# Per-token scales: from identity products into a bank to a DRAM row loaded for every partition

## The chip, the cores and the metric

One core of one Trainium2 chip runs the kernel. The metric is device microseconds of one execution. Three runs of the kernel before gave a median of 2810.96 us (2810.95 to 2812.11). A profile is one further execution, recorded by the hardware profiler.

## The reference

A one-layer encoder block on x of 2048 tokens by 1024 features, in float32. What matters here is where a per-token scale is multiplied in:

```python
def rms_norm(x, g):
    y = xf * lax.rsqrt(jnp.mean(xf * xf, axis=-1, keepdims=True) + NORM_EPS)
    return (y * g).astype(x.dtype)

def hybrid_layer(...):
    xn = rms_norm(x, mix_norm_g)
    proj = xn @ w_in                       # attention, mLSTM and gate inputs
    ...
    x = x + y @ w_out
    hn = rms_norm(x, ffn_norm_g)
    x = x + jnp.square(jax.nn.relu(hn @ w_up)) @ w_down
    return x
```

A last RMSNorm closes the block. The scale of a token is one number, the same for all 1024 features. The kernel keeps features on the 128 partitions and tokens along the free dimension, so it needs the scales of 512 tokens as a row of 512 values, the same in every partition.

## The kernel before

The 2048 tokens are four blocks `b` of T = 512; blocks 0 and 1 form the first span (s = 0), 2 and 3 the second. Matrices are float32, each split into a high and a low part (tiles `r` and `wsp`), and each product is three matmuls of 128x512: L644 to L646 in plain tiles and in the FFN's down projection, L727 and L755 where a two-by-two block scheme with seven products (`quad`) is used. There are 10,680 of these large matmuls. Attention and mLSTM work of smaller shapes (L1344, L1375, L1406, L1630 to L1702) is put between them.

The work is written as generators, each of which says on which engine its next step runs and for how long. `Flow` (L96) runs them against a clock per engine and so sets TensorE's order. `Order` (L225) then takes the finished instructions, keeps TensorE's order, and sets that of VectorE, ScalarE, GpSimd and SP by due times and by when their inputs are ready, with a margin (2.5 us behind a DMA). The result is a fixed order on every engine. All DMAs are issued by SP, one after the other; each takes the next of eight semaphores, and an SP instruction that waits holds up those behind it.

SBUF tiles come from pools: `tmp` (6 tiles of 128x516), `ctx` (16), `bias` (2), `wraw` (4, raw weights) and `wsp` (3, split weights). PSUM has 8 banks (`self.banks`) of 128x512.

Scales are computed as a [128, 4] tile, tokens on partitions: token t·128 + p of a block is at partition p, column t. To turn that into a row in all partitions, the kernel multiplies a column, broadcast to 128x128, with the identity, four times, into one bank. It does so in three places:

- `norm_in` (L1026), for blocks 0 and 1: squares and sums of x, a product with ones (L1059), mean and eps (L1063), power −0.5 on GpSimd (L1067), the four products (L1074). Eight `scale_in` (L1154) then multiply x by gain and row on VectorE (L1161), send the result to DRAM (`xn`) and split it for the block's products.
- `stats_far` and `rows_far` (L1085, L1107), for blocks 2 and 3: the scale is computed from x loaded with tokens on partitions (L1096 to L1105) and kept in `r_far`; later the products (L1115) go into a bank and ScalarE copies it to a `bias` tile (L1118), which the loads of x multiply by (L1788).
- `norm_mid` (L2092) and `residual` (L2174): the FFN's input isn't scaled; the factor (`mid`, L2110) is applied to the residual instead. In each span's down projection, `residual` goes through four groups (half of the features, block h). Per group: four products (L2183) into a bank; then for each of four feature tiles x2 is loaded into a `tmp` tile (L2198), multiplied by the bank (L2200) and added to the accumulator (L2204). The next group starts when the multiplies are done.

The final RMSNorm (`final`, L2239) needs the finished accumulators: squares (L2284), their sum (L2287), a product with ones (L2309), transposes (L2340), and scaled outputs (L2349 on ScalarE or L2351 on VectorE), stored by L2355. `split_now` (L579) splits weights on ScalarE (L583) and VectorE (L585).

Of the kernel before, what the change touches and what calls it, by code (L numbers as in the profile page):

```python
# [28 lines left out]
ALU = mybir.AluOpType  # L29

P = 128
D = 1024
S = 2048
T = 512
# [338 lines left out]
class Layer:  # L373
# [652 lines left out]
    def norm_in(self, b):  # L1026
        fl, nc = self.fl, self.nc
        B = self.blk[b]
        r = self.rr["x"]
        xt, ev = [], [Event() for _ in range(KT)]  # L1030
        if b == 0:
            (tot,) = yield "get", self.ctx, 1
            xt = yield "get", self.ctx, KT
            B["xg"] = yield "get", self.rpool, KT
            B["xs"] = yield "get", self.rpool, KT
            fl.set(B["xs_ev"])
            for k in range(KT):
                fl.spawn(self.square_in(b, k, xt[k], tot, ev), 0)
        else:
            (tot,) = yield "get", self.ctx, 1  # L1040
            for k in range(KT):
                if k > 0:
                    (x,) = yield "get", self.ctx, 1
                else:
                    x = tot
                yield "sp", 900, 2000
                nc.sync.dma_start(x[:, :T], self.io["xt"][b, k])
                yield "act", act_ns(T)
                nc.scalar.square(x[:, :T], x[:, :T])
                if k > 0:  # L1050
                    yield "dve", dve_ns(T)
                    nc.vector.tensor_add(tot[:, :T], tot[:, :T], x[:, :T])
                    fl.put(self.ctx, x)
                fl.set(ev[k])
        yield "wait", ev
        (bk,) = yield "get", self.banks, 1
        yield "pe", 900
        for t in range(NT):
            nc.tensor.matmul(bk[:, 2 * t:2 * t + 2], tot[:, t * P:(t + 1) * P], self.ones,  # L1059
                             start=True, stop=True)  # L1060
        fl.put(self.ctx, tot)
        yield "dve", 75
        nc.vector.tensor_scalar(r, bk[:, :2 * NT].rearrange("p (t a) -> p t a", a=2)[:, :, 0], 1.0 / D, EPS,  # L1063
                                op0=ALU.mult, op1=ALU.add)
        fl.put(self.banks, bk)
        yield "pool", 960
        nc.gpsimd.tensor_tensor(r, r, self.half, op=ALU.pow)  # L1067
        if b == 0:
            fl.set(self.ev_r)
            yield "wait", [self.ev_const]  # L1070
        (bk,) = yield "get", self.banks, 1
        yield "pe", 1080
        for t in range(NT):
            nc.tensor.matmul(bk[:, t * P:(t + 1) * P], r[:, t:t + 1].to_broadcast([P, P]), self.ident,  # L1074
                             start=True, stop=True)
        done = [Event() for _ in range(KT)]
        for k in range(KT):
            if b > 0:
                (x,) = yield "get", self.ctx, 1
                xt.append(x)  # L1080
            fl.spawn(self.scale_in(b, k, xt[k], bk, done[k]), 2)
        yield "wait", done
        fl.put(self.banks, bk)

    def stats_far(self):  # L1085

        fl, nc = self.fl, self.nc
        for b in (2, 3):
            r, q = self.rfar[b - 2], self.rq
            for t in range(NT):  # L1090
                for g in range(2):
                    (x,) = yield "get", self.temp, 1
                    x5 = x[:, :T]
                    yield "sp", 900, 2000
                    row = b * T + t * P
                    nc.sync.dma_start(x5, self.io["x"][row:row + P, g * T:g * T + T])  # L1096
                    yield "act", act_ns(T, ap=1)
                    nc.scalar.activation(x5, x5, AF.Square, accum_out=q[:, g, t:t + 1])
                    fl.put(self.temp, x)
            yield "dve", 75  # L1100
            nc.vector.tensor_add(r, q[:, 0], q[:, 1])
            yield "dve", 75
            nc.vector.tensor_scalar(r, r, 1.0 / D, EPS, op0=ALU.mult, op1=ALU.add)
            yield "pool", 960
            nc.gpsimd.tensor_tensor(r, r, self.half, op=ALU.pow)  # L1105

    def rows_far(self, ready, read):  # L1107

        fl, nc = self.fl, self.nc
        got = yield "get", self.bias, 2  # L1110
        for b in range(2):
            (bk,) = yield "get", self.banks, 1
            yield "pe", 1080
            for t in range(NT):
                nc.tensor.matmul(bk[:, t * P:(t + 1) * P], self.rfar[b][:, t:t + 1].to_broadcast([P, P]),  # L1115
                                 self.ident, start=True, stop=True)
            yield "act", act_ns(512, True)
            nc.scalar.copy(got[b][:, :T], bk)  # L1118
            fl.put(self.banks, bk)
            self.rows[b] = got[b][:, :T]  # L1120
        fl.set(ready)
        yield "wait", read
        fl.put(self.bias, *got)
# [27 lines left out]
            fl.put(self.temp, tmp)  # L1151
        fl.set(ev[k])

    def scale_in(self, b, k, slot, bk, ev):  # L1154
        fl, nc = self.fl, self.nc
        x = slot[:, :T]
        if b > 0:
            yield "sp", 900, 2000
            nc.sync.dma_start(x, self.io["xt"][b, k])
        yield "dve", dve_ns(574)  # L1160
        nc.vector.scalar_tensor_tensor(x, x, self.gcol[:, 0, k:k + 1], bk, op0=ALU.mult, op1=ALU.mult)  # L1161
        fl.set(ev)
        fl.spawn(self.store(self.xnd[b].ap()[k], x, self.xn_kept[b][k]), 2)
        if b > 0:
            B = self.blk[b]
            if k > 0:
                yield "wait", [B["x_room"][k - 1]]
            B["xs"] += yield "get", self.rpool, 1
            fl.set(B["x_room"][k])
            if k == KT - 1:  # L1170
                fl.set(B["xs_ev"])
        yield from self.split(x, self.blk[b]["xs"][k])
        fl.set(self.blk[b]["xn" if b > 0 else "xs_done"][k])
        yield "wait", [self.xn_kept[b][k]]
        fl.put(self.ctx, slot)
# [916 lines left out]
    def norm_mid(self, s, h):  # L2092

        fl, nc, B = self.fl, self.nc, self.blk[2 * s + h]
        (tot,) = yield "get", self.bias, 1
        summed = [Event() for _ in range(KT)]
        yield "wait", B["x2"]
        for j in range(KT):
            (x,) = yield "get", self.sc, 1
            fl.spawn(self.square_mid(s, h, j, x, tot[:, :512], summed), 3)  # L2100
        yield "wait", summed
        (bk,) = yield "get", self.banks, 1
        yield "pe", 900
        for t in range(NT):
            nc.tensor.matmul(bk[:, 2 * t:2 * t + 2], tot[:, t * P:(t + 1) * P], self.ones,
                             start=True, stop=True)
        fl.put(self.bias, tot)
        m, e = self.mid[h], self.mid2[h]
        yield "dve", 75
        nc.vector.tensor_scalar(m, bk[:, :2 * NT].rearrange("p (t a) -> p t a", a=2)[:, :, 0], 1.0 / D, EPS,  # L2110
                                op0=ALU.mult, op1=ALU.add)
        fl.put(self.banks, bk)
        yield "dve", 75
        nc.vector.scalar_tensor_tensor(e, m, EPS, m, op0=ALU.mult, op1=ALU.mult)
        fl.set(B["mid"])

    def square_mid(self, s, h, j, x, tot, summed):
# [56 lines left out]
    def residual(self, s):  # L2174
# [2 lines left out]
        done = []  # L2177
        for o, h in ((0, 0), (4, 1), (0, 1), (4, 0)):
            yield "wait", [self.blk[2 * s + h]["mid"], self.acc_ev[s][o, h]]
            (bk,) = yield "get", self.banks, 1  # L2180
            yield "pe", 432
            for t in range(NT):
                nc.tensor.matmul(bk[:, t * P:(t + 1) * P], self.mid[h][:, t:t + 1].to_broadcast([P, P]),  # L2183
                                 self.ident, start=True, stop=True)
            done = []
            for j in range(o, o + 4):
                yield "wait", [self.acc_ev[s][j, h]]
                (x,) = yield "get", self.temp, 1
                done.append(Event())
                fl.spawn(self.residual1(s, j, h, bk, x, done[-1]), 2)  # L2190
            yield "wait", done
            fl.put(self.banks, bk)

    def residual1(self, s, j, h, bk, x, done):
        V = self.nc.vector
        x5 = x[:, :512]
        yield "sp", 900, 2000
        self.nc.sync.dma_start(x5, self.x2d[2 * s + h].ap()[j])  # L2198
        yield "dve", dve_ns(512)
        V.tensor_mul(x5, x5, bk)  # L2200
        self.fl.set(done)
        a = self.acc[s][j, h][:, :512]
        yield "dve", dve_ns(512)
# [159 lines left out]
    def build(self):  # L2363
# [14 lines left out]
        self.ypd = [f32d(f"yp{b}", KT, P, T) for b in range(NB)]  # L2378
        self.fin = [f32d(f"fin{h}", 4, P, T) for h in range(2)]
        self.ud = f32d("u", 4, 7, 4, P, T)  # L2380
        self.wi = 0
        self.y3 = [{}, {}]
        self.wtile = {}
# [112 lines left out]
```

## Time and profile before

| | |
|---|---|
| median of three runs | 2810.96 us |
| the profiled execution | 2811.24 us |
| its span, first to last instruction | 2809.5 us |
| mean granted TensorE clock | 0.999 |
| moved by DMA | 662.41 MB, mean 236 GB/s |
| HBM read, written | 462.63 MB, 197.13 MB |

How to read the lines that follow. PE is TensorE's matmuls, PEld its weight loads (they overlap with matmuls), DVE is VectorE, ACT ScalarE, POOL GpSimd, SP the queue that issues the DMAs. A group line gives source line, engine, operation, output tile `<-` input tiles, shapes and count, then busy time, the mean of one in ns, and the idle time before with what ended it. A line of the timeline or of the chain begins with start and length in us. A line of the waits has "engine tile line `<-` what it waited for: us in total, times, longest". A view of one source line gives min/median/max in ns, then first and last start. A DMA line ends with KB each and the median us from issue to landing.

### The profile page before, as it was taken

To read this page: it belongs to the slowest core of one execution; us is meant where nothing else is said; L and a number is where in the kernel's file an instruction comes from. 1 tells how busy PE (TensorE), PEld (TensorE's weight loads), DVE (VectorE), ACT (ScalarE), POOL (GpSimd) and SP (SyncE) were. 2 spreads that over 40 slices of the span, in tenths; PEclk is the share of its full clock that TensorE was granted. 3 is DMA by queue.
4 is the path that set the end of the run, shared out by engine and by line. 5 is a ranking of instruction groups with operands and counts; after the bars stand their busy time and mean duration, and the time that the engine had idled before them with its cause. 6 is when DMAs were issued, how large, how long until landed. Compare 5 with 4: busy or idle time off the path is not lost.

```text
span 2809.5 us, 39519 instructions
## 1 busy us (share of the span) xinstructions
PE 2785.5 (99%) x13528; PEld 2331.6 (83%) x13528; DVE 2042.4 (73%) x3742; ACT 1528.2 (54%) x2642; POOL 50.3 (2%) x100
## 2 busy tenths in 40 slices
PE   9999999999999999999999999999999999999998
PEld 7887888888878878888888888888888888888887
DVE  7796789668896866886676788889888644555565
ACT  5564577544354535575555566566645655554444
POOL 0010001000000000000000000000000000000000
PEclk9999999999999999999999999999999999999999
DMA  7957758768756667588878776688687655666563
GB/s 270 290 193 252 225 157 287 242 221 301 244 185 207 239 235 262 187 292 315 290 274 283 262 235 206 222 266 261 206 272 254 210 187 200 218 228 205 191 224 133
DMA packets 317737, 662.41 MB, mean 236 GB/s; under 512 B 35552, under 2 KB 62304, under 8 KB 317536
## 3 DMA queue, kind: packets, MB, share of 16 engines
q1 hardware_dynamic: 317536, 659.90, 70.1%
q8 instruction: 106, 1.74, 0.3%
q14 instruction: 95, 0.78, 0.1%
HBM read 462.63 MB, written 197.13 MB: 235 GB/s over the span
## 4 chain that ended last, share of the span: by engine, by line
PE 95%; DMA 2%; DVE 2%; ACT 1%; issue 1%; SPq 0%; POOLq 0%; DVEq 0%; ACTq 0%
PE bank L727 44%; PE bank L644 12%; PE bank L645 12%; PE bank L646 12%; PE bank L1344 3%; PE bank L1375 2%; PE bank L1406 2%; PE bank L755 2%; DVE wsp L585 0%; PE bank L1667 0%; PE bank L1668 0%; PE bank L2340 0%; PE bank L1669 0%; PE bank L1653 0%; DMA r<-mfar 0%
## 5 line engine op out<-in xcount | busy, mean ns | idle before, releaser
L727 PE MATMUL bank<-r,wsp 128*128 128x512 f32 x5544 | 1263.6, 390 | 1.6 <-ACT r L1182 1.1
L727 PEld LDWEIGHTS bank<-r,wsp 128*128 128x128 f32 x5544 | 1038.6, 188 | 221.1 <-DVE ctx L1834 3.1
L585 DVE TENSOR_TENSOR wsp<-wraw,wsp 128x1024 fp32r<-128x1024 f32 x459 | 561.1, 1223 | 375.3 <-ACT wsp L583 357.6
L583 ACT CAST wsp<-wraw 128x1024 fp32r<-128x1024 f32 x459 | 482.4, 1051 | 498.4 <-PE bank L727 224.8
L644 PE MATMUL bank<-r,wsp 128*128 128x512 f32 x1472 | 590.0, 401 | 1.6 <-ACT r L1180 1.6
L645 PE MATMUL bank<-r,wsp 128*128 128x512 f32 x1472 | 575.8, 391 | 0.4 <-DVE r L1185 0.4
L646 PE MATMUL bank<-r,wsp 128*128 128x512 f32 x1472 | 575.1, 391 | 0.0
L646 PEld LDWEIGHTS bank<-r,wsp 128*128 128x128 f32 x1472 | 276.3, 188 | 59.2
L644 PEld LDWEIGHTS bank<-r,wsp 128*128 128x128 f32 x1472 | 277.0, 188 | 50.0 <-ACT r L1180 2.4
L645 PEld LDWEIGHTS bank<-r,wsp 128*128 128x128 f32 x1472 | 277.2, 188 | 48.4 <-DVE r L1185 1.0
L1834 DVE TENSOR_TENSOR ctx<-bank,ctx 128x512 f32<-128x512 f32 x186 | 127.1, 688 | 100.7 <-PE bank L727 100.5
L1185 DVE TENSOR_TENSOR r<-r 128x512 fp32r<-128x512 f32 x264 | 174.2, 690 | 30.4 <-ACT r L1180 29.1
L1180 ACT CAST r<-r 128x512 fp32r<-128x512 f32 x264 | 157.7, 621 | 56.3 <-DMA r<-u 49.4
L1826 ACT COPY ctx<-bank 128x512 f32<-128x512 f32 x186 | 108.0, 582 | 71.5 <-PE bank L727 67.5
L1390 ACT ACTIVATE sc<-sc,scs 128x640 f32<-128x640 f32 (+4 forms) x128 | 97.5, 763 | 65.8 <-DVE scs L1387 55.7
L2164 ACT ACTIVATE ctx<-ctx 128x512 f32<-128x512 f32 x96 | 60.6, 631 | 100.7 <-DVE ctx L1834 100.7
L1411 DVE TENSOR_TENSOR r<-bank,r 128x512 fp32r<-128x512 f32 (+1 forms) x168 | 96.5, 596 | 17.6 <-ACT r L1409 16.7
L1381 DVE CUSTOM_DVE_ANT_0 sc<-bank,bias 128x320 f32<-128x320 f32 (+3 forms) x240 | 103.3, 462 | 6.2 <-PE bank L1375 4.9
L1344 PE MATMUL bank<-r,r 128*128 128x256 f32 (+1 forms) x672 | 105.9, 279 | 0.2 <-DVE r L1411 0.2
L1344 PEld LDWEIGHTS bank<-r,r 128*128 128x128 f32 x672 | 98.3, 189 | 9.2 <-DVE r L1411 0.5
L1409 ACT CAST r<-bank 128x512 fp32r<-128x512 f32 (+1 forms) x168 | 81.1, 516 | 35.4 <-PE bank L1406 31.0
L602 DVE TENSOR_TENSOR wraw<-wraw,wraw 128x1024 f32<-128x1024 f32 x76 | 92.9, 1223 | 2.0
(247 smaller groups left out, 2764.5 us busy)
## 6 DMA issues: line engine op xcount, KB each, us to landing
wraw<-in_wf SPq DMA_DIRECT2D x178, 512.0 KB, 4.3
wraw<-wsum SPq DMA_DIRECT2D x136, 512.0 KB, 4.1
r<-u SPq DMA_DIRECT2D x224, 256.0 KB, 4.2
wraw<-in_w SPq DMA_DIRECT2D x88, 512.0 KB, 5.0
u<-ctx SPq DMA_DIRECT2D x128, 256.0 KB, 2.5
ctx<-in_wf SPq DMA_DIRECT2D x112, 256.0 KB, 4.6
wsum<-ctx SPq DMA_DIRECT2D x112, 256.0 KB, 4.1
u<-tmp SPq DMA_DIRECT2D x96, 256.0 KB, 3.7
```

What stands on the lines that cost most here:

```text
L583: nc.scalar.copy(w[:, 0], raw)
L585: nc.vector.tensor_sub(w[:, 1], raw, w[:, 0].bitcast(F32))
L644: mm(ps, lh, rh, start=first, stop=False)
L645: mm(ps, lh, rl, start=False, stop=False)
L646: mm(ps, ll, rh, start=False, stop=last)
L727: mm(ps, wv[:, x, k, n], a[:, y], start=new and k == 0 and x == y == 0, stop=k == 3 and x == 1, skip_group_check=True)
L1180: self.nc.scalar.copy(dst[:, 0], src)
L1185: self.nc.vector.tensor_sub(dst[:, 1], src, dst[:, 0].bitcast(F32))
L1344: nc.tensor.matmul(bk[:, c0:c0 + w], st, sl[:, x, o:o + w], start=n == 0, stop=n == total - 1)
L1381: nc.vector.tensor_tensor_reduce(out=e[:, x * w:x * w + w], in0=bks[x][:, :w], in1=br[:, j0 + x * w:j0 + x * w + w], op0=ALU.add, op1=ALU. ...
L1826: nc.scalar.copy(t[:, o:o + 512], ps)
L1834: nc.vector.tensor_add(t[:, o:o + 512], ps, t[:, o:o + 512])
```

## The change

The row no longer goes through TensorE and a bank. The [128, 4] tile is stored to a small DRAM tensor as 512 consecutive values (`row_out`), and the row is loaded into all 128 partitions of an SBUF tile by a DMA whose source has a step of 0 over the partitions (`row_in`). There is one DRAM row for block 1's input scale, one each for blocks 2 and 3, and one for each of the four blocks' `mid`. Block 0 keeps its products. `residual` loads the row anew for each of its groups, into a `tmp` tile that is held until the group's multiplies are done; `norm_in` of block 1 holds one too. `rows_far` loads straight into the `bias` tiles, without a bank and a copy.

```diff
@@ norm_in
-        (bk,) = yield "get", self.banks, 1
-        yield "pe", 1080
-        for t in range(NT):
-            nc.tensor.matmul(bk[:, t * P:(t + 1) * P], r[:, t:t + 1].to_broadcast([P, P]), self.ident,
-                             start=True, stop=True)
+            (bk,) = yield "get", self.banks, 1
+            row = bk
+            yield "pe", 1080
+            for t in range(NT):
+                nc.tensor.matmul(bk[:, t * P:(t + 1) * P], r[:, t:t + 1].to_broadcast([P, P]), self.ident,
+                                 start=True, stop=True)
+        else:
+            yield from self.row_out("in1", r)
+            (bk,) = yield "get", self.temp, 1
+            row = bk[:, :T]
+            yield from self.row_in("in1", row)
...
-        fl.put(self.banks, bk)
+        fl.put(self.banks if b == 0 else self.temp, bk)
+
+    def row_out(self, name, src):
+        yield "sp", 500, 2000
+        self.nc.sync.dma_start(self.rowd[name].ap().rearrange("(t p) -> p t", p=P), src)
+
+    def row_in(self, name, dst):
+        yield "sp", 900, 2000
+        self.nc.sync.dma_start(dst, bass.AP(self.rowd[name], 0, [[0, P], [1, T]]))
@@ stats_far
             nc.gpsimd.tensor_tensor(r, r, self.half, op=ALU.pow)
+            yield from self.row_out(f"in{b}", r)
@@ rows_far
-            (bk,) = yield "get", self.banks, 1
-            yield "pe", 1080
-            for t in range(NT):
-                nc.tensor.matmul(bk[:, t * P:(t + 1) * P], self.rfar[b][:, t:t + 1].to_broadcast([P, P]),
-                                 self.ident, start=True, stop=True)
-            yield "act", act_ns(512, True)
-            nc.scalar.copy(got[b][:, :T], bk)
-            fl.put(self.banks, bk)
+            yield from self.row_in(f"in{b + 2}", got[b][:, :T])
@@ scale_in
-        nc.vector.scalar_tensor_tensor(x, x, self.gcol[:, 0, k:k + 1], bk, op0=ALU.mult, op1=ALU.mult)
+        nc.vector.scalar_tensor_tensor(x, x, self.gcol[:, 0, k:k + 1], row, op0=ALU.mult, op1=ALU.mult)
@@ norm_mid
+        yield from self.row_out(f"mid{2 * s + h}", m)
         fl.set(B["mid"])
@@ residual
-            (bk,) = yield "get", self.banks, 1
-            yield "pe", 432
-            for t in range(NT):
-                nc.tensor.matmul(bk[:, t * P:(t + 1) * P], self.mid[h][:, t:t + 1].to_broadcast([P, P]),
-                                 self.ident, start=True, stop=True)
+            (row,) = yield "get", self.temp, 1
+            yield from self.row_in(f"mid{2 * s + h}", row[:, :T])
...
-            fl.put(self.banks, bk)
+            fl.put(self.temp, row)
@@ residual1
-        V.tensor_mul(x5, x5, bk)
+        V.tensor_mul(x5, x5, row)
```

More of the change, by code (lines that the diff above doesn't have):

```diff
@@ L1080, in norm_in @@
                 xt.append(x)
-            fl.spawn(self.scale_in(b, k, xt[k], bk, done[k]), 2)
+            fl.spawn(self.scale_in(b, k, xt[k], row, done[k]), 2)
         yield "wait", done
-        fl.put(self.banks, bk)
+        fl.put(self.banks if b == 0 else self.temp, bk)
[5 more added lines that the diff above has]
+        self.nc.sync.dma_start(dst, bass.AP(self.rowd[name], 0, [[0, P], [1, T]]))
     def stats_far(self):
@@ L1152, in square_in, with scale_in @@
         fl.set(ev[k])
-    def scale_in(self, b, k, slot, bk, ev):
+    def scale_in(self, b, k, slot, row, ev):
         fl, nc = self.fl, self.nc
@@ L2189, in residual, with residual1 @@
                 done.append(Event())
-                fl.spawn(self.residual1(s, j, h, bk, x, done[-1]), 2)
+                fl.spawn(self.residual1(s, j, h, row[:, :T], x, done[-1]), 2)
             yield "wait", done
-            fl.put(self.banks, bk)
-    def residual1(self, s, j, h, bk, x, done):
+            fl.put(self.temp, row)
+    def residual1(self, s, j, h, row, x, done):
         V = self.nc.vector
@@ L2380, in build @@
         self.ud = f32d("u", 4, 7, 4, P, T)
+        self.rowd = {n: f32d("row" + n, T) for n in ("in1", "in2", "in3", "mid0", "mid1", "mid2", "mid3")}
         self.wi = 0
```

## The prediction

> **What bounds the kernel now.** I read the page first, for which engine is full and whether it also carries the chain that ended last.
>
> ```profile
> span 2809.5 us, 39519 instructions
> ...
> PE 2785.5 (99%) x13528; PEld 2331.6 (83%) x13528; DVE 2042.4 (73%) x3742; ACT 1528.2 (54%) x2642; POOL 50.3 (2%) x100
> ...
> q1 hardware_dynamic: 317536, 659.90, 70.1%
> ...
> PE 95%; DMA 2%; DVE 2%; ACT 1%; issue 1%; SPq 0%; POOLq 0%; DVEq 0%; ACTq 0%
> ```
>
> TensorE is busy 99% of the span and is 95% of the chain. Since a share is a mean over stages, the second view was busy time by stretch: the start, the middle, the end.
>
> ```profile
> 0.00:12.00 12.00, 5.41 (x14) 4.26 (x15) 5.78 (x19) 7.65 (x11) 0.20 (x4) 1.00 0.82 294
> ...
> 40.00:2790.00 2750.00, 2741.43 (x13311) 2295.80 (x13310) 2008.31 (x3675) 1499.49 (x2598) 47.49 (x90) 1.00 0.71 236
> 2790.00:2810.00 20.00, 10.66 (x72) 9.35 (x71) 6.36 (x10) 6.49 (x10) 1.01 (x1) 0.84 0.28 105
> ```
>
> Columns are the stretch, its length, then busy time of PE, PEld, DVE, ACT, POOL, the granted clock, the DMA share and GB/s. In the 2750 us of the middle PE lacks 2750 − 2741.43 = 8.6 us; 6.6 us are missing at the start and 9.3 at the end. The third view, TensorE's waits, says who ended those 8.6.
>
> ```profile
> PE bank L644 <- ACT r L1136: 6.6, 1, 6.6
> PE bank L755 <- DVE ctx L1834: 2.4, 2, 2.0
> PE bank L1642 <- DMA r<-mfar: 1.6, 1, 1.6
> ```
>
> The first is the start; the other nine rows are small (2.4 us and less) and scattered, and none names a scale product or a user of one. So in the middle a microsecond of instructions taken off TensorE is worth a microsecond, if the rest arrives in time.
>
> **What is removed.** The line views count the products of the row with the identity; the b = 0 half of L1074 stays.
>
> ```profile
> L1074 PE MATMUL bank<-const,r_x x16: 271/275/275, 33.1 to 180.0; 128*128 128x128 f32 x16
> L1115 PE MATMUL bank<-const,r_far x16: 271/275/275, 747.6 to 751.4; 128*128 128x128 f32 x16
> L2183 PE MATMUL bank<-const,mid x64: 271/275/276, 1645.7 to 2740.9; 128*128 128x128 f32 x64
> ```
>
> A call of four products shows as 8 MATMULs. 8 of L1074, 16 of L1115 and 64 of L2183 go: 88 MATMULs, 11 groups of 8. The built program of the change agrees: 44 products fewer, the 10,680 large matmuls unchanged. The 275 ns are latency, since the products overlap; what a group takes from TensorE is its piece of the chain:
>
> ```profile
> 179.34 0.89 PE bank L1074 x8
> ...
> 747.79 0.89 PE bank L1115 x8
> 750.75 0.89 PE bank L1115 x8
> ...
> 1645.86 0.89 PE bank L2183 x8
> ```
>
> TensorE's timeline gives the same by starts, and shows how the 0.89 is made up.
>
> ```profile
> 1645.47 0.39 PE L644 MATMUL bank<-r,wsp 128*128 128x512 f32 x1
> 1645.70 1.05 PE L2183 MATMUL bank<-const,mid 128*128 128x128 f32 x8
> 1646.51 0.48 PE L645 MATMUL bank<-r,wsp 128*128 128x512 f32 x1
> 1646.82 0.39 PE L646 MATMUL bank<-r,wsp 128*128 128x512 f32 x1
> ```
>
> The next matmul starts 0.81 us after the group, and its own slot is 0.31 instead of the usual 0.23: 0.81 + 0.08 = 0.89. The built order returns from small products to large ones 356 times, before 366, so the 0.08 goes too, about ten times. Removed from TensorE: 11 × 0.89 = **9.8 us**. Two ACT copies of L1118 (0.59 each) go as well; ACT is 54% busy, worth nothing.
>
> **What is added.** Seven stores of a [128, 4] scale tile to a DRAM row and eleven loads of that row to 128 partitions, all on SP. Neither shape is in the trace. The store scatters 512 values of 4 bytes; the load is 128 pieces of 2 KB from one address. Nearest rows:
>
> ```profile
> bias<-in_rb SPq DMA_DIRECT2D x32, 320.0 KB, 4.6
> ...
> mix<-tmp SPq DMA_DIRECT2D x64, 64.0 KB, 3.7
> ...
> r<-mvfar SPq DMA_DIRECT2D x16, 256.0 KB, 5.6
> ...
> L1589 SPq DMA_DIRECT2D r<-mvfar x16: 370/384/645, 70.4 to 1854.0; - x16
> ```
>
> L1278 (bias) reads overlapping pieces of one short row into all partitions, which is the nearest to the new load: 4.6 us from issue to landing. For the store I take between 3.7 (a small store to DRAM) and 5.6 (a load in as many pieces, 512 of 512 bytes). The lower end for either is that it costs nothing, the upper the whole flight on the path. Issue is 0.37 to 0.65 us each: 18 × 0.65 = 12 us at most on a queue that issues 2,166 DMAs in 2809.5 us, one in 1.30 us. The loads add 11 × 0.26 = 2.9 MB to 660.
>
> [...]
>
> **Is the flight covered?** Three places. First, block 1's input scale:
>
> ```profile
> 172.10 1.36 POOL L1067 TENSOR_TENSOR r_x<-r_x,half 128x4 f32<-128x4 f32 x1 [15.47 <-ACT sc L1390]
> ...
> 170.84 0.64 SPq L1159 DMA_DIRECT2D ctx<-in_xt  x1
> 178.01 0.33 SPq L2087 DMA_DIRECT2D mfar<-ctx  x1
> 179.91 0.33 SPq L565 DMA_DIRECT2D wraw<-in_w  x1
> ...
> 199.55 0.75 DVE L1161 SCALAR_TENSOR_TENSOR ctx<-ctx,gcol,bank 128x512 f32<-128x512 f32 x1
> ```
>
> The built order puts the store between SP's rows at 170.84 and 178.01 and the load right behind the latter. SP idles from 171.5 to 178.0, so the store goes at 173.5 when the power ends, and is down at 173.5 + 3.7 to 5.6 = 177.2 to 179.1. SP waits there up to 0.8 us past the mfar store, and the weight load behind it slips by that and an issue slot. Weights have room: what ends ACT's waits before the split (L583) is TensorE giving up the last tile, not the load.
>
> ```profile
> ACT wsp L583 <- PE bank L727: 224.8, 154, 4.4
> ```
>
> The row is down by about 185; its first reader ran at 199.55: 14 us to spare. Second, blocks 2 and 3:
>
> ```profile
> L1105 POOL TENSOR_TENSOR r_far<-r_far,half x2: 1006/1006/1007, 498.9 to 524.8; 128x4 f32<-128x4 f32 x2
> ```
>
> The scale exists at 526 and the products came at 747: over 200 us of room. One load stands four DMAs behind its store (4 × 1.30 = 5.2 us against a flight of 3.7 to 5.6), so SP may wait 0.4 us. Third, the eight rows of the FFN residual:
>
> ```profile
> L2110 DVE TENSOR_SCALAR mid<-bank x4: 156/158/164, 1364.3 to 2301.5; 128x4 f32<-128x4 f32 x4
> ...
> L2198 SPq DMA_DIRECT2D tmp<-x x32: 319/326/538, 1632.3 to 2720.2; - x32
> ...
> 1855.00:1935.00 80.00, 80.00 (x453) 69.54 (x452) 69.23 (x168) 48.64 (x103) 3.72 (x6) 1.00 0.88 284
> ```
>
> The stores have hundreds of microseconds. In the built order each row load stands ahead of its group's first full load of x (L2198) or close by, so the multiply (L2200) waits for x anyhow. What changes is room: the row holds one of six tmp tiles for the group's life where it held a bank. The tight stretch is 1855 to 1935, three of the groups, with DVE at 69.23/80 = 87% and DMA at 0.88. Three loads of 0.26 MB at 284 GB/s are 2.8 us there if they delay everything, 0 if they fit the gaps; I take 0, since TensorE waits for a DMA once in the whole run (1.6 us above).
>
> DVE reads the row from SBUF instead of a bank:
>
> ```profile
> L1161 DVE SCALAR_TENSOR_TENSOR ctx<-ctx,gcol,bank 128x512 f32<-128x512 f32 x16 | 11.4, 741 | 0.0
> L1788 DVE SCALAR_TENSOR_TENSOR ctx<-ctx,gcol,bias 128x512 f32<-128x512 f32 x8 | 5.7, 748 | 0.8 <-ACT bias L1118 0.8
> ```
>
> 7 ns × 40 instructions = 0.3 us, hidden behind TensorE.
>
> The planner also lays the small work anew. TensorE's waits of 8.6 us in the middle can shrink or grow; I take no change, with ends of −3 (a third gone) and +8.6 (doubled). The last stretch has the same instructions in the same order, so the 9.3 us at the end stay.
>
> **Sum.** The profiled execution took 2811.24 us, 1.74 over its span and 0.28 over the median of 2810.96. 2811.24 − 9.8 = 2801.4; on the median's scale **2801.2 us**, −0.35%.
>
> **Rivals.** *Given back in the tight stretch.* DVE or DMA sets the pace in 1855 to 1935, so the three groups there earn nothing (+2.7) and their loads cost (+2.8): 2801.2 + 5.5 = 2806.7. For it: 87% and 88%. Against: TensorE has no gap there (80.00 of 80).
>
> *Exposed round trips, slower than before.* Multiplies stand in DVE's fixed order; if a row is late, all of DVE's work behind it is, the weight splits (L585) among it, and TensorE stops. It takes the row load waiting for a tmp tile. Likeliest for the three groups at 1860 to 1925 and the last two at 2714 and 2740. Price 5.0 us each (the landing of an x load into tmp, bound from 4.6 above): 5 × 5.0 − 9.8 = +15.2, 2826. It is slower by over 0.2% from 15.4/5.0, four, exposures on. Against it: the groups lie 20 us and more apart,
>
> ```profile
> 2694.88 0.89 PE bank L2183 x8
> 2714.84 0.89 PE bank L2183 x8
> 2740.25 0.89 PE bank L2183 x8
> ```
>
> and the built order finishes the attention's small products of the first span earlier than before, not later, so tmp isn't starved. [...]
>
> *A slow scatter.* DMAs take eight semaphores in turn, so a store in flight longer than eight issues (8 × 1.30 = 10.4 us) stops SP. With 15 us each: 7 × 4.6 − 9.8 = +22, 2833; it is slower by over 0.2% from 10.4 + 15.4/7 = 12.6 us on. Against: twice 5.6 us would still be hardly more than 10.4.
>
> *It doesn't do what it says.* The count of products leaves no room; 2811.
>
> **Numbers.** Forecast 0.77, given back 0.13, exposed 0.06, slow scatter 0.03, no effect 0.01. A difference under 0.2% (5.6 us) can't be told from none here: faster 0.77, same 0.14, slower 0.09. The range runs from 2801.2 − 3 = 2798 to just past the given-back case, 2808.
>
> **What would show it.** Right: 88 MATMULs fewer, TensorE's busy time 2775 to 2777, its waits in the middle under 12 us, store and load landing in 3 to 6 us, the readers of the rows idle for other reasons. Wrong: DVE waits at L2200 that end with the row's DMA, SP waits on the row store of several microseconds, or new TensorE waits in 1850 to 1940 or behind 2690.

## The result, and the profile after

The changed kernel takes 2828.95 us (median of four runs, 2825.74 to 2831.03) against 2811.53 for the kernel before (four runs, 2810.95 to 2812.67): the ratio of the runs on record is 1.0057, with a 95% interval of 1.0045 to 1.0070 (the two medians alone give 1.0062). It became 17.4 us slower where 9.8 us less were forecast. One later run of the kernel before, 3475.51 us at a granted clock of 0.752, is left out of every ratio. The profiled execution took 2831.03 us, 19.8 more than the profiled one of before.

The page of the kernel after, in the order in which the page of before was read: span, engines, chain of waits.

```profile
span 2829.2 us, 39333 instructions
...
PE 2783.6 (98%) x13440; PEld 2326.7 (82%) x13440; DVE 2042.2 (72%) x3744; ACT 1522.9 (54%) x2638; POOL 50.2 (2%) x100
...
PE 82%; DVE 7%; DMA 7%; ACT 2%; issue 1%; SPq 0%; POOLq 0%; DVEq 0%; ACTq 0%
```

The 88 matmuls are gone (13,528 to 13,440), and TensorE is busy 1.9 us less in a span 19.7 us longer, so it now stands idle about 22 us more, and part of its busy time is slower. The chain that ended last has lost 13 points of TensorE to DVE and DMA. TensorE's waits say where, in the columns engine, tile and line, what ended the wait, then total, times and longest in us:

```profile
PE bank L727 <- DVE ctx L1843: 17.8, 3, 10.8
PE bank L644 <- ACT r L1145: 6.1, 1, 6.1
```

The second row is the start, as before. The first is new: 10.8 us at one place, and by the timeline 6.7 us at a second. Busy time by stretch puts them at 542 and 1418 us (columns as before: stretch, length, PE, PEld, DVE, ACT, POOL, granted clock, DMA share, GB/s). In the kernel before, TensorE was full in both:

```profile
530.00:546.00 16.00, 16.00 (x71) 13.03 (x70) 10.10 (x11) 6.31 (x9) 0.00 (x0) 1.00 0.49 165
...
1396.00:1426.00 30.00, 30.00 (x133) 24.62 (x132) 23.03 (x28) 17.10 (x25) 0.00 (x0) 1.00 0.76 265
```

After:

```profile
530.00:546.00 16.00, 12.23 (x54) 9.75 (x53) 5.14 (x8) 4.32 (x8) 1.01 (x1) 0.96 0.84 203
553.00:566.00 13.00, 12.95 (x46) 10.45 (x47) 4.87 (x5) 4.83 (x7) 0.00 (x0) 0.79 0.60 201
...
1396.00:1426.00 30.00, 23.26 (x101) 18.82 (x100) 14.82 (x18) 11.19 (x17) 0.00 (x0) 0.93 0.83 266
1426.00:1440.00 14.00, 14.00 (x57) 11.41 (x56) 10.98 (x15) 8.36 (x13) 0.00 (x0) 0.90 0.74 273
```

```profile
546.00:553.00 7.00, 0.00 (x0) 0.00 (x0) 6.21 (x9) 2.19 (x3) 0.00 (x0) 0.50 0.82 303
```

Behind each stall the granted clock is low for a while: 0.79 for 13 us, 0.90 for 14. The 0.79 is a mean of half and full speed:

```profile
553.00:558.30 5.30, 5.25 (x12) 4.12 (x13) 1.82 (x2) 2.10 (x3) 0.00 (x0) 0.50 0.83 289
558.40:566.00 7.60, 7.60 (x35) 6.26 (x34) 3.05 (x3) 2.73 (x4) 0.00 (x0) 1.00 0.44 142
```

The first stall therefore costs more than 10.8: at 0.79, 13 × 0.21 = 2.7 us more, together 13.5.

The chain of waits at the first stall, in order of time (start, length, what), leads from TensorE back to loads that have nothing to do with the change:

```profile
524.22 8.73 DMA gate<-ctx
...
533.01 9.34 DMA ctx<-in_wf
...
545.56 5.51 DMA wraw<-in_wf
...
552.31 0.70 DVE ctx L1843
...
553.05 22.06 PE bank L727 x85
```

L547 loads pieces of the FFN's weights, and VectorE subtracts them from each other in L552 and L602. VectorE's order is fixed, so a late load there stops all of VectorE, the addition of finished banks (L1843) included; TensorE then has no free bank. The load took 9.34 us; VectorE stood 9.2 us in front of L552, and TensorE 10.8 us in front of L727.

At the second stall the chain has the same kind of links, and one more:

```profile
1391.28 9.31 DMA u<-tmp
1400.66 7.90 DMA wsum<-ctx
1408.58 0.70 DVE ctx L552
1410.69 6.06 DMA ctx<-in_wf
...
1418.10 0.69 DVE ctx L1843
```

The store of this place was issued at 1391.71, so u<-tmp had been issued 0.4 us ahead of it and was late all the same. SP issued eight DMAs from 1391.28 to 1396.21; the ninth, wsum<-ctx, had to wait for the semaphore of the first until u<-tmp had landed. SP's waits from 1370 to 1426 us name it:

```profile
SPq L2096 <- DMA u<-tmp: 3.6, 1, 3.6
```

So at the second stall the late transfers reach TensorE partly through SP, which stood still for 3.6 us. How much of the 6.7 us this stop makes wasn't separated.

The kernel before has these medians for the same transfers, from its list of DMA issues (KB each, us from issue to landing):

```profile
wraw<-in_wf SPq DMA_DIRECT2D x178, 512.0 KB, 4.3
...
ctx<-in_wf SPq DMA_DIRECT2D x112, 256.0 KB, 4.6
...
tmp<-gate SPq DMA_DIRECT2D x56, 256.0 KB, 4.4
```

And this is the DMA view of the kernel after from 532 to 544 us, in 40 slices of 0.3 us. The second store of blocks 2 and 3 is issued at 532.00.

```profile
GB/s 396 423 430 389 437 444 356 329 362 363 369 186 178 191 123 89 34 55 41 27 14 20 20 48 20 20 34 27 68 34 7 55 14 14 27 75 164 137 68 109
...
tmp<-gate SPq DMA_DIRECT2D x2, 256.0 KB, 12.0
wraw<-in_wf SPq DMA_DIRECT2D x1, 512.0 KB, 12.7
...
ctx<-in_wf SPq DMA_DIRECT2D x1, 256.0 KB, 9.3
...
rowin<-r_far SPq DMA_DIRECT2D x1, 2.0 KB, 10.2
```

From slice 12 to slice 36, 7.5 us, the queues move 7 to 191 GB/s, and below 76 from slice 17 on, while four large transfers, issued behind the store of 2 KB, are under way. They land in 9 to 13 us, where the medians of the kernel before are 4.3 to 4.6. The store is down at 532.0 + 10.2 = 542.2, ctx<-in_wf at 542.35, and the others behind it. VectorE's waits, after and before, count what that made of L552:

```profile
DVE ctx L552 <- DMA ctx<-in_wf: 24.5, 7, 9.2
```

```profile
DVE ctx L552 <- DMA ctx<-in_wf: 9.8, 4, 2.9
```

All seven stores were slow, by the view of their source line; the row loads were a little slower than the 4.6 us taken for them (3.7 to 7.5, 5.9 in the median).

```profile
DMA to landing us min/median/max: 8.9/10.6/11.8
```

Where the time came from, by the start of the n-th large matmul, after minus before:

```
n        at (before)   offset
1440     487.6 us      +0.1
1920     597           +13.1     stores at 515.6 and 532.0
2640     764           +9.8
5280     1380          +10.9
5640     1462          +19.4     stores at 1375.7 and 1391.7
6000     (1550)        +19.2
7800     (2130)        +23.8     four groups of row loads, first span
9600     2542          +23.7
10560    2767          +18.2
last instruction       +19.8
```

The two steps are 13.0 and 8.5 us, together 21.5. What the removed products gave back is seen between them. From +13.1 to +9.8 only some 1.9 belong to the two groups of blocks 2 and 3 (746 to 753 us); the other 1.4 lie at 717 to 731 us, where the stores alone, which keep all products, fall by 1.7 too. The last four groups give +23.7 to the +19.8 of the end; the +18.2 in between comes and goes with the order there, as it does with the loads alone (+3.3, +1.5, +3.2), which keep their products.

### The profile page after: what moved, and what is told of

Read it like the earlier page. It is cut to its first block, busy times and chain, and to the rows that moved or that the text cites. A ratio compares the mean times of both kernels' runs of the same rounds, so it can differ in the third digit from the quotient of the medians.

```text
span 2829.2 us, 39333 instructions
## 1 busy us (share of the span) xinstructions
PE 2783.6 (98%) x13440; PEld 2326.7 (82%) x13440; DVE 2042.2 (72%) x3744; ACT 1522.9 (54%) x2638; POOL 50.2 (2%) x100
## 4 chain that ended last, share of the span: by engine, by line
PE 82%; DVE 7%; DMA 7%; ACT 2%; issue 1%; SPq 0%; POOLq 0%; DVEq 0%; ACTq 0%
PE bank L727 36%; PE bank L644 12%; PE bank L645 11%; PE bank L646 11%; PE bank L1353 2%; PE bank L1384 2%; PE bank L1415 2%; PE bank L755 2%; DVE wsp L585 2%; DMA wsum<-ctx 1%; DMA ctx<-in_wf 1%; ACT wsp L583 1%; DVE ctx L552 1%; DVE r L1194 1%; DMA gate<-ctx 0%
## 5 line engine op out<-in xcount | busy, mean ns | idle before, releaser
L727 PE MATMUL bank<-r,wsp 128*128 128x512 f32 x5544 | 1268.3, 390 | 19.4 <-DVE ctx L1843 17.8
L727 PEld LDWEIGHTS bank<-r,wsp 128*128 128x128 f32 x5544 | 1041.6, 188 | 241.4 <-DVE ctx L1843 21.6
L1843 DVE TENSOR_TENSOR ctx<-bank,ctx 128x512 f32<-128x512 f32 x186 | 126.9, 688 | 94.7 <-PE bank L727 94.4
L1420 DVE TENSOR_TENSOR r<-bank,r 128x512 fp32r<-128x512 f32 (+1 forms) x168 | 96.4, 596 | 20.4 <-ACT r L1418 19.8
L602 DVE TENSOR_TENSOR wraw<-wraw,wraw 128x1024 f32<-128x1024 f32 x76 | 92.9, 1224 | 10.6 <-DMA wsum<-wraw 8.4
```

The source lines that it names most:

```text
L727: mm(ps, wv[:, x, k, n], a[:, y], start=new and k == 0 and x == y == 0, stop=k == 3 and x == 1, skip_group_check=True)
L1843: nc.vector.tensor_add(t[:, o:o + 512], ps, t[:, o:o + 512])
```

## The experiments

Three theories stood against each other. S: the scattered store takes long and holds up the transfers that are in the DMA queues with it. W: SP stands before a row load, waiting for its store, and everything behind it on SP is late. L: it's the row loads, the `tmp` tile that they hold, and the order that the planner lays anew. W is plausible from SP's waits in front of the row loads (L1098) of the kernel after:

```profile
SPq L1098 <- DMA rowin<-r_far: 8.4, 2, 7.4
...
SPq L1098 <- DMA rowin<-r_x: 4.0, 1, 4.0
```

### Stores alone

To the kernel before the seven stores of the change are added, read by nobody; all products stay.

```diff
@@ norm_in
+        else:
+            yield from self.row_out("in1", r)
@@ stats_far
+            yield from self.row_out(f"in{b}", r)
@@ norm_mid
+        yield from self.row_out(f"mid{2 * s + h}", m)
```

> The kernel before with the seven row stores added, which nothing reads; the products stay on TensorE. Theory S (the store of 512 pieces of 4 bytes holds up the DMA queues for about 10 us, so transfers issued around it land late, and TensorE stops): 15 to 24 us slower than before, from the two steps of 13.4 us (near 542) and 8.5 us (near 1418) in the change's trace; stores land in 9 to 12 us, and transfers issued just behind them in 8 us or more. Rival W (SP stands still in front of the load that waits for the store): no load, so no wait; within 3 us of before. Rival L (the loads, the tmp tile they hold, and the order laid anew): within 3 us of before.

Measured: 2827.6 us (median of four) against 2812.11 (25 runs), ratio 1.0054, 1.0039 to 1.0070: +15.5 us. Three views of this kernel show what the kernel after showed: the store's landing, TensorE's waits, and the stretches behind the second store, which is issued at 530.0 here.

```profile
DMA to landing us min/median/max: 9.2/9.7/12.0
```

```profile
PE bank L727 <- DVE ctx L1842: 11.6, 2, 7.4
```

```profile
530.00:546.00 16.00, 13.43 (x60) 10.79 (x58) 4.93 (x6) 3.61 (x6) 0.01 (x1) 1.00 0.61 139
546.00:551.00 5.00, 0.17 (x1) 0.17 (x2) 4.50 (x5) 1.12 (x3) 0.00 (x0) 0.55 0.70 234
```

The steps in the offset are +10.2 at 542 to 570 and +7.0 at 1400 to 1435, the end +15.2. The late load of the first step is another one than in the kernel after: tmp<-gate, issued 1.8 us behind the store, which VectorE's L933 waits for. From the chain:

```profile
531.83 10.53 DMA tmp<-gate
...
542.37 0.04 DVE tmp L933
```

No row load exists here, so SP never waits in front of one; it does stop for 4.1 us on a late u<-tmp, from 1394 to 1398, as in the kernel after. So W isn't needed, and the stores alone make 15.5 of the 27.2 us that have to be explained (17.4 lost and 9.8 not gained). That the order is laid anew with the stores in it isn't excluded by this run; the runs with other pieces below do that.

### Loads alone

Eleven row loads are added to the kernel before, from an input that lies ready, into the tiles of the change and held as long as there; nothing reads them, and all products stay.

```diff
+            (extra,) = yield "get", self.temp, 1
+            yield from self.row_in(extra[:, :T])
...
+            fl.put(self.temp, extra)
...
+    def row_in(self, dst):
+        self.nc.sync.dma_start(dst, bass.AP(self.io["rb"].tensor, 0, [[0, P], [1, T]]))
```

> The kernel before with the eleven row loads added (from an input row of the same size, into the tiles that the change uses, held as long as the change holds them); the products stay and are what is multiplied by. Theory S: within 3 us of before. Rival W: within 3 us. Rival L: 5 to 20 us slower, in the stretch from 1550 to 2150 above all, where the change loses some 5 us beside its two steps.

Measured: 2814.99 us (ten) against 2812.11, ratio 1.0012, 1.0003 to 1.0021: +2.9 us. That is inside the 3 us that S and W left for it and below the 5 that L gave. The offset grows by 4.0 us between the 6000th and the 7800th large matmul, the FFN of the first span, and is small elsewhere. L exists, but alone it is the smaller part.

### The change with a store in four pieces

The change, but the [128, 4] tile is first transposed to [4, 128] by one product with the identity and copied out of the bank by ScalarE, so that the store writes four pieces of 512 bytes.

```diff
     def row_out(self, name, src):
...
+        (bk,) = yield "get", self.banks, 1
...
+        nc.tensor.matmul(bk[:NT, :P], src, self.ident, start=True, stop=True)
+        (rt,) = yield "get", self.temp, 1
...
+        nc.scalar.copy(rt[:NT, :P], bk[:NT, :P])
...
-        self.nc.sync.dma_start(self.rowd[name].ap().rearrange("(t p) -> p t", p=P), src)
+        nc.sync.dma_start(self.rowd[name].ap().rearrange("(t p) -> t p", p=P), rt[:NT, :P])
```

> The change with the scale tile transposed on TensorE first (one product with the identity for a [4, 128] result, copied to SBUF by ScalarE), so that the store is 4 pieces of 512 bytes; the loads and the waits stay. Theory S: 11 groups of 0.89 us go, 7 single products of about 0.3 us come, so 2811 - 9.8 + 2 = about 2803, up to 2808 with the loss between 1550 and 2150; stores land in 2 to 5 us. Rival W: SP still waits for the stores in front of the loads, so the step near 542 stays at 5 us or more: 2809 to 2815. Rival L: over 2815.

Measured: 2808.59 us (ten) against 2812.11, ratio 0.9987, 0.9977 to 0.9997. Both steps are gone with the scattered stores. That alone doesn't tell S from W, since a quicker store also shortens SP's wait; the stores alone did. The landing of these stores isn't in the trace. The time is 0.6 us above the upper end that S gave, since the first span's FFN costs more than I had allowed. The stretch from 1550 to 2130 us, first of the kernel before, then of this one (columns as above):

```profile
1550.00:2130.00 580.00, 577.83 (x3176) 497.38 (x3175) 487.76 (x1127) 333.62 (x672) 16.95 (x38) 1.00 0.74 240
```

```profile
1550.00:2130.00 580.00, 574.70 (x3128) 493.13 (x3127) 481.18 (x1119) 331.60 (x670) 17.13 (x38) 0.99 0.74 238
```

TensorE lacks 2.2 us there before and 5.3 now, in several waits of 1.3 us and less. The offset grows by 4.7 us over this stretch although four groups of products (3.6) are gone from it, so the row loads and the new order cost 8.3 there. 3.1 of it is this idle time. Two short stretches at half the clock, where the kernel before had none, make another 2 × 3.3 × 0.5 = 3.3:

```profile
1559.10:1562.40 3.30, 3.30 (x11) 2.63 (x11) 2.15 (x3) 1.07 (x2) 0.00 (x0) 0.50 1.04 405
1811.70:1815.00 3.30, 3.30 (x13) 2.93 (x12) 3.06 (x13) 0.00 (x0) 0.00 (x0) 0.50 0.09 22
```

The remaining 1.9 us stay open.

### Stores in pieces of 16 bytes

As the stores alone, but each partition writes its four values side by side: 128 pieces of 16 bytes (the row's order is then another; nobody reads it). Of the store's line only the end changes:

```diff
-.rearrange("(t p) -> p t", p=P), src)
+.rearrange("(p t) -> p t", p=P), src)
```

> As the run with stores alone, but the four values of a partition lie side by side in DRAM: 128 pieces of 16 bytes in place of 512 of 4. If the number of pieces sets the time (S by count): stores land in 3 to 5 us, and the kernel is 0 to 6 us slower than before. If any store of pieces this small does it (S by smallness, or neighbours sharing a line in DRAM): landings of 9 to 12 us again and 15 to 24 us slower.

Measured: 2812.55 us (ten) against 2812.11, ratio 1.0002, 0.9992 to 1.0011, no difference. The landing:

```profile
DMA to landing us min/median/max: 1.4/4.1/6.2
```

A quarter of the pieces takes half of the time or less and does no harm. It leaves open whether the number of pieces decides or that they lie close together.

### The same 512 pieces, spread

As the stores alone: 512 pieces of 4 bytes, but 512 bytes apart in DRAM (again read by nobody). The end of the store's line:

```diff
-.rearrange("(t p) -> p t", p=P), src)
+.rearrange("(t p c) -> p t c", p=P, c=P)[:, :, 0], src)
```

> As the run with stores alone, with the same 512 pieces of 4 bytes, each now 512 bytes from the next in DRAM instead of side by side. If the number of pieces sets the time: landings of 9 to 12 us and 12 to 18 us slower than before, as with the pieces side by side. If it is the pieces that share a line of DRAM which wait for each other: landings of 4 to 6 us and 0 to 5 us slower.

Measured: 2812.74 us (ten) against 2813.47 (27 runs), ratio 1.0000, 0.9991 to 1.0009. The page counts exactly as many packets as with the packed stores, whose line is the same to the last digit, and yet the landing is another than 9.7:

```profile
DMA packets 321433, 662.43 MB, mean 235 GB/s; under 512 B 39248, under 2 KB 66000, under 8 KB 321232
```

```profile
DMA to landing us min/median/max: 2.0/3.8/5.1
```

The DMA view for the 12 us from 527, with the same store issued at 527.3, has the queues at 184 to 410 GB/s until there is nothing to move, and no plateau near 20:

```profile
GB/s 362 260 348 246 184 198 335 341 370 329 322 322 295 370 362 239 266 300 294 355 410 273 96 0 0 0 0 0 0 0 0 0 0 0 150 205 328 328 437 219
...
rowin<-r_far SPq DMA_DIRECT2D x1, 2.0 KB, 4.4
```

TensorE is full in the two stretches in which it stood with the packed stores:

```profile
530.00:546.00 16.00, 16.00 (x72) 13.01 (x71) 9.80 (x11) 5.56 (x9) 0.00 (x0) 1.00 0.49 172
...
1396.00:1426.00 30.00, 30.00 (x134) 24.62 (x133) 21.43 (x26) 15.22 (x23) 0.00 (x0) 1.00 0.77 279
```

By their traces, the stores alone, the stores in pieces of 16 bytes and the spread ones run the same instructions in the same order on every engine; they differ only in where the store's values lie in DRAM and in how many pieces it has. So neither an added instruction nor the new order makes the 15.5 us, and it isn't the count of packets either (321,433 with the packed stores and with the spread ones): the two steps came only with 4-byte pieces that lie next to each other in DRAM (landings of 9.7 us in the median, against 3.8 spread and 4.1 in pieces of 16 bytes).

### How close is too close

The same with 16 and with 64 bytes between pieces (c = 4 and c = 16 in the line above), one execution each.

> Stores alone again, 512 pieces of 4 bytes, 16 bytes apart (they were slow 4 bytes apart and quick 512 bytes apart). If pieces wait for each other in a block of a fixed size of DRAM, each piece taking its turn, a quarter as many share a block: landings of 4 to 6 us, as with 128 pieces of 16 bytes. If any two pieces in one block of 64 bytes or more slow the whole store: 9 to 12 us again.

> The same with 64 bytes from piece to piece. If the block in which pieces wait for each other is 64 bytes or smaller: landings of 2 to 5 us, as 512 bytes apart. If it is larger (256 or 512 bytes): between those and the run 16 bytes apart.

Measured, against 2810.53 us for the kernel before: 2811.44 with 16 bytes, 2816.27 with 64. The second isn't a result on the time: runs of the spread stores alone lie between 2809.6 and 2818.8, and its offset has no step at a store. The landings, 16 bytes first, then 64:

```profile
DMA to landing us min/median/max: 2.9/5.1/7.3
```

```profile
DMA to landing us min/median/max: 1.9/4.0/5.8
```

Block 1's store, which goes when the queues are quiet (a DMA share of 0.25 and 76 GB/s from 173 to 183 us in the kernel after), orders them best by its own record, one store in each run: 9.4 us packed, 2.9 at 16 bytes, 1.9 at 64, 2.0 at 512. Most of the cost is gone at 16 bytes from piece to piece, the rest at 64, and beyond that no difference is seen; 32 bytes weren't tried. Both expectations came true by the medians (5.1 and 4.0), but blocks of 64 bytes whose pieces are written in turn aren't shown by this: the 128 pieces of 16 bytes also lie four to each 64 bytes, as the 4-byte pieces 16 bytes apart do, and block 1's store landed in 1.4 us there, not in 2.9. What makes the neighbours slow stays open.

### The products kept for blocks 2 and 3

The change, with `stats_far` and `rows_far` as before: two of the seven stores, those at 515.6 and 532.0 us, are gone.

```diff
@@ stats_far
-            yield from self.row_out(f"in{b}", r)
@@ rows_far
-            yield from self.row_in(f"in{b + 2}", got[b][:, :T])
+            (bk,) = yield "get", self.banks, 1
...
+            for t in range(NT):
+                nc.tensor.matmul(bk[:, t * P:(t + 1) * P], self.rfar[b][:, t:t + 1].to_broadcast([P, P]),
+                                 self.ident, start=True, stop=True)
...
+            nc.scalar.copy(got[b][:, :T], bk)
```

> The change with its part for blocks 2 and 3 undone: their two rows go through products and a bank again, so two of the seven scattered stores (those near 516 and 532) and two loads are gone. Theory S (a scattered store holds up the DMA queues, and what it costs depends on what is late behind it): the step of 13.4 us near 542 goes and two groups of 0.89 us come back, so 2829 - 13.4 + 1.8 = 2817; the step near 1418 stays. If all seven stores cost alike (17 / 7 = 2.5 us each): 2829 - 5 + 1.8 = 2826.

Measured: 2814.34 us (ten) against 2813.47, ratio 1.0001, 0.9992 to 1.0010. By S it was to be 2817, and 2826 if each store cost alike; the measured time is 2.7 us below the former. Without a store at 532 the step at 542 is gone, and the second stays, with +7.2:

```profile
530.00:546.00 16.00, 16.00 (x72) 12.99 (x71) 11.81 (x14) 6.47 (x9) 0.00 (x0) 1.00 0.63 217
...
1396.00:1426.00 30.00, 25.81 (x101) 20.75 (x100) 19.41 (x25) 13.26 (x20) 0.00 (x0) 0.89 0.72 279
```

Each against the kernel before of its own series, the change is 17.4 us slower and this one 0.9, so these two stores, with their two loads and the order laid for them, cost 16.5 us, though two groups of products go in exchange. The three stores at 175, 2307 and 2325 cost nothing that the offset shows. The two chains above suggest why: a store costs where instructions on TensorE's path are about to need transfers that are in flight with it. What was in flight beside the three cheap ones wasn't compared.

### Rows only where there is room

The store in four pieces, with rows for blocks 2 and 3 and for the second span's residual only; block 1 and the first span keep their products. Two of the places:

```diff
-        yield from self.row_out(f"mid{2 * s + h}", m)
+        if s > 0:
+            yield from self.row_out(f"mid{2 * s + h}", m)
...
+            (row,) = yield "get", self.temp if s > 0 else self.banks, 1
```

> The four-piece store, with rows only where the runs show room: for blocks 2 and 3 and for the four residual groups of the second span; block 1 and the first span's residual keep their products. Six groups of 0.89 us go, four transposes of about 0.3 us come: 2811.5 - 5.3 + 1.2 = 2807.4. If the loads and the held tmp tile of the first span cost the 3 us that the loads alone did, this is 1 to 2 us faster than the four-piece store everywhere; if they cost nothing there, it is 2 us slower than that one, at 2810 or more.

Measured: 2807.37 us (eleven) against 2813.47, ratio 0.9975, 0.9966 to 0.9984. It is faster than both kernels (its runs lie between 2805.0 and 2810.0). That it meets the expected 2807.4 so closely is luck in part: the sum started from 2811.5, and of this series the kernel before took 2813.47, so 6.1 us were gained where 4.1 were expected. Against the four-piece store everywhere (0.9987 of the kernel before, and 0.9975 here) it is ahead, but the two intervals overlap. In the stretch from 1550 to 2130 us, where the four-piece store lacked 5.3 us, TensorE is as busy as in the kernel before (577.98 us of 580 against 577.83).

## Why the prediction was wrong

**What bounds the kernel: right.** TensorE's idle time decided, and the loss is idle time of TensorE (10.8 and 6.7 us) with the slow clock behind it (0.79 for 13 us, 0.90 for 14).

**What is removed: right.** 88 matmuls are gone, and the offset falls by about 0.9 us a group where nothing else happens. Against "TensorE's busy time 2775 to 2777" stand 2783.6 us, some 8 more than 2785.5 − 9.8: behind the stalls matmuls run at a lower clock, which counts as busy and by the rows at 553 and 1426 us is about 4 of them (13 × 0.21 and 14 × 0.10).

**What is added: the step that failed.** "For the store I take between 3.7 (a small store to DRAM) and 5.6 (a load in as many pieces, 512 of 512 bytes)." The stores took 8.9 to 11.8, and the run with the spread pieces, in which they take 2.0 to 5.1, is as fast as the kernel before. Both neighbours were bounds for another thing: the first writes 64 KB, the second reads pieces of 512 bytes, and no row of the trace has pieces as small as 4 bytes side by side in a write. The upper end was then no upper end. By the spread stores, which have the same count of packets and land in 3.8 us, the count isn't the reason. Pieces of 4 bytes landed in 3.8 to 4.0 us when 64 bytes or more lay between them, so the size of the piece doesn't decide it either.

**Is the flight covered? The question was too narrow.** I asked for each store only whether its own reader could wait. It could: the view of the residual's multiplies (L2207 in the kernel after, 32 of them, 686 ns in the median) lists no wait in front of any of them.

For blocks 2 and 3 there were over 200 us of room, and these two stores were the dearest of all. What was late was the load issued 1 us behind the store, ctx<-in_wf, and VectorE's subtraction that waits for it. I had priced the queue in bytes and in issue slots, never as time in which a transfer holds up the ones around it. SP's own waits were under-priced too: 7.4 us in front of a row load of blocks 2 and 3 where I gave 0.4, and 4.0 at block 1 (whose store took 8.9 us) where I gave 0.8. The latter cost nothing that the offset shows, as forecast; the former isn't on the chain that ended last.

**The residual's rows: a term mis-sized.** I took 0 with an end of 2.8 for the tight stretch and 0 for the new order. The mechanism (room for tiles, the order laid anew) was named; the first span's FFN lost 8.3 us in the four-piece version and about 8.2 in the change (+4.6 in the offset from 1550 to 2132, with 3.6 of products gone). That is more than "given back" (5.5) allowed. The loads alone cost some 4.0 of it; the rest, with products gone and a new order, wasn't taken apart further.

**The rivals.** The slow scatter came nearest, with a flight of 9 to 12 us, against which I had held that even twice 5.6 is hardly more than 10.4; but its way to the time was another: it let SP stop at the eighth semaphore, from 10.4 us on, so that the flights measured, 10.6 in the median, would have cost nearly nothing, and it had all seven stores cost alike. In the trace only the four around 515 to 532 and 1376 to 1392 cost anything. SP did stop at its semaphores, which the rival had right, but sooner than at 10.4 us: that figure takes the mean of one issue in 1.30 us, and from 1391.28 to 1396.21 SP issued eight in 4.9 us, so that a flight of 9.3 us stopped it. The mean hid the stage here too. The stop was caused by a neighbour of the store, not by the store, and the step at 542 doesn't need it: there the late loads are waited for by VectorE itself. The exposed round trips gave 2826, near the time, by a mechanism that isn't there.

**The sum as measured**, in the profiled executions: −9.8 (products) + 13.0 + 8.5 (the two steps) + 8.2 (first span) = +19.9, against 19.8; smaller moves of the offset, up to 1.4 us either way, about cancel. The parts measured alone don't add up to the change: stores +15.5 and loads +2.9 less 9.8 make +8.6, against +17.4. In the change the two steps are larger by about 4 us than with the stores alone (21.5 against 17.2) and the first span by about 4 (8.2 against 4.0). The order in the change is another one; what in it makes both larger stays open.

## What to carry to other kernels

A column of values that must become a row in DRAM is not to be written in 4-byte pieces side by side: transposing it on chip first worked here (2808.59 us against 2812.11), and the same 2 KB that took 9.7 us in that form took 3.8 to 4.1 in pieces of 16 bytes, or with the 4-byte pieces 64 bytes and more apart. An added transfer is priced not only by who waits for it but by who waits for the transfers in flight with it: look at what is issued from 1 us ahead of it to some 9 us behind it, and put it where that isn't needed soon. In the kernel after, around the store at 515.63 us, a wsum<-ctx issued 0.96 us ahead of it took 9.1 us (median before 4.1) and a gate<-ctx issued 8.6 us behind it 8.7 (2.4). A duration bounded by neighbours of another form (a read for a write, 512 bytes for 4) is no bound, and a rival should be given its chance accordingly.

## What the runs showed of the hardware

- Stores of 512 values of 4 bytes to consecutive addresses landed in 8.9 to 12.0 us (the change and the stores alone), against 2.0 to 5.1 with the same number of pieces 512 bytes apart. What makes neighbouring pieces slow, and whether it takes pieces of one queue or of several, wasn't tried.
- Such a store of 2 KB brought the queues down to 7 to 75 GB/s for 6 us, with four other transfers of 256 and 512 KB under way, which landed in 9.3 to 12.8 us. A transfer issued 0.4 us ahead of such a store was late as well (9.3 us, against a median of 3.7 for u<-tmp before).
- While TensorE stood from 546 to 553 us the granted clock was 0.50, and over the next 13 us it was 0.79 in the mean: 0.50 for 5.3 us, with 12 matmuls, then 1.00, with 35 in 7.6 us. Behind the second stall it was 0.90 over 14 us, with 57 matmuls where the kernel before had 64 at 1.00. As an estimate from these means, the slow clock cost 13 × 0.21 = 2.7 us behind the first stall and 14 × 0.10 = 1.4 behind the second. What made the clock fall and return isn't shown.
